# Two pools for the operands of an output projection, its first products in another order, and the keys of two key halves loaded into tiles that are free

## The chip, the core and the metric

The kernel runs on one core of one Trainium2 chip, in one launch. The metric is device time in microseconds (us). The kernel before takes 1855.24 us, the median of 3 runs (1855.01 to 1856.59). The engines are PE (TensorE, matrix products), DVE (VectorE), ACT (ScalarE), POOL (GpSimd) and SP (SyncE, which here only issues DMA transfers). ACT issues transfers as well, and such an issue stands in ACT's own instruction order.

## The reference, cut to what matters

One layer of a hybrid diffusion transformer, float32: 512 latent tokens of width 1024, 256 context tokens.

```python
def reference(x, c, ctx, ...):
    z, xbc, dtr, pl, q, k, v = project(h, sh1, sc1, norm1_g, w_in)
    ssd_l = ssd_mixer(...)                      # 512 x 1024
    na  = neighbourhood_attention(q, k, v, kc, vc, rpb)     # 512 x 512
    mix = concatenate([ssd_l, pool_mixer(pl, ...), na]) @ w_out   # 512 x 2048 @ 2048 x 1024
    h = h + g1 * mix
    u = rmsnorm(h, norm2_g) * (1 + sc2) + sh2
    h = h + g2 * peer_ffn(u, peer_wq, peer_keys, peer_u, peer_v)
    return rmsnorm(h, final_g)

def peer_ffn(u, w_q, sub_keys, u_tab, v_tab):
    q = (t @ w_q).reshape(n_tok, 8, 2, 128)
    s = einsum('thid,hikd->thik', q, sub_keys)  # 16 key halves of 128 keys each
    v1, i1 = top_k(s[:, :, 0], 16); v2, i2 = top_k(s[:, :, 1], 16)
    ...  # 16 of the 256 pairs per head and token, then softmax, gelu(u_tab[idx] . u), sum of v_tab[idx]
```

## The kernel before

A float32 product A·B is done as three fast products: each operand is split into a high part (fp32r; ACT, `split`, L177) and a low part, which is what the high part leaves (a subtraction, L180, on DVE or POOL), and high·high, high·low and low·high are summed in PSUM (`mm3`, L187 to L189; the trace names the operands in the other order). The names end in `h` and `l`: `wh` and `wl` are the parts of a 512 KB piece of weights, which SP loads into a tile `wraw` (L208).

**Output projection beside attention.** The mixed rows have three sources. The SSD part is normalised and transposed on PE, DVE writes it (L910, tiles `y` and `xsn`), SP stores it to `mix_d` in DRAM (L914), and it is loaded again (`s` items) and split into `mAh`, `mAl`. The pooled part lies in `mix_d` already; it is loaded in two pieces (`p4`, `p5`) and split into the first half of `mBh`, `mBl`. Attention writes the second half of those tiles. Tiles `h` (the residual, 4 loads of 512 KB from `x`, L1193), `g1r`, `mBh`, `mBl`, `mAh` and `mAl` are in one pool, `o1`. The pool reaches over the place where `xsn` lay, so the first write to it waits until `xsn` has been stored.

The order of instructions is written by hand: `at(step, f)` puts a piece of work at a step, `before` puts it ahead of what is there, and `run` issues steps 61 onward (`O0 = A0 = 61`) one by one. An engine takes its instructions in that order. Attention takes a pair of heads and a column group (`m` = 0 to 15) every 4 steps: scores (L1026), minimum (L1035, L1036), exponential (L1043), division (L1048, L1049, every second one on POOL), transposes (L1056), copy (L1061), values (L1074). Its biases `nb` are loaded by ACT (L967), its values `vl` by SP (L1015). Between them stand `i_high` and `i_low`, the splits of the next item (`w4, p4, p5, w5, s0, ...`), and `o_part(kk, t)`: 6 products (two halves of a 256-row piece, three each) for 128 tokens and one piece `kk` of `w_out`. The pieces come in the order 4, 5, 0, 1, 2, 3, the four `o_part(4, t)` at steps 62, 62, 63 and 64. A low part that is done frees the item's `wraw`, and the next load waits for that.

**Norm and the step to PEER.** After the output projection, `norm2` (L1250) scales each 128 tokens, `norm2_T` transposes (L1258), `norm2_split` splits into `u2h` and `u2l` in two halves (`q4`). `u_block` computes the products `pu` with 128-expert pieces of `peer_ut`. `q_part` computes a query half (24 products). Two Gelu results `otmp` are stored to `act_d` by ACT (L1363). Then `scores(hi, pq)` (L1406 to L1413): ACT loads the 128 keys of key half `hi`, copies the query half into `qk`, PE multiplies (L1411), ACT copies into `sc`, DVE picks the best 16. `keys`, `qk` and `sc` lie in pool `sc1`, over the place of the tiles `otmp`. `idxG`, `gG` (128 x 128) and `mod`, `cst` are tiles that exist at this time. Up to the end PE then works through the 128 expert pieces (`pu` and `pv`, from about 650 us).

Of the kernel before, what the change touches and what calls it, by code (L numbers as in the profile page):

```python
# [7 lines left out]
F32 = mybir.dt.float32  # L8
F32R = mybir.dt.float32r
# [3 lines left out]
AF = mybir.ActivationFunctionType  # L13
# [4 lines left out]
P = 128  # L18
D = 1024
# [131 lines left out]
def build(tc, A, out, dbg=None):  # L151
# [4 lines left out]
    def dump(name, ap):  # L156
        if name in dbg:
            nc.sync.dma_start(dbg[name], ap)
# [16 lines left out]
    def split(hi, lo, full, eng=None, lows=None):  # L175

        S.activation(hi, full, AF.Copy)  # L177

        def low():
            (eng or V).tensor_tensor(lo, full, hi.bitcast(F32), ALU.subtract)  # L180
        if lows is None:
            low()
        else:
            lows.append(low)
# [474 lines left out]
    def at(step, f, *a):  # L659
        plan.setdefault(step, []).append((f, a))  # L660
# [310 lines left out]
    def i_high(i):  # L971
        kind, n = items[i]
        raw = iraws.pop(i)
        if kind == "w":
            ispls[n] = wspl(raw, 2, None, ilows)
        elif kind == "p":
            ks = slice(2 * n - 8, 2 * n - 6)
            split(mix["h"][:, ks, :].rearrange("p k t -> p (k t)"), mix["l"][:, ks, :].rearrange("p k t -> p (k t)"), raw, None, ilows)
        else:
            ts_ = slice(n * P, (n + 1) * P)  # L980
            split(mix["ah"][:, :, ts_], mix["al"][:, :, ts_], raw.rearrange("p (k t) -> p k t", k=8), None, ilows)
# [131 lines left out]
    ws.extend(wop, "O", 1, 2, "right")  # L1113
    op = Pools()
    o1 = op.sb("o1", side="right")
    pso = Pools()
    psO = pso.ps("psO", bufs=4)
    h = o1.tile([P, NX, D], F32, name="h")
    g1r = o1.tile([P, D], F32, name="g1r")
    mBh = o1.tile([P, 8, SEQ], F32R, name="mBh")  # L1120
    mBl = o1.tile([P, 8, SEQ], F32R, name="mBl")
    mAh = o1.tile([P, 8, SEQ], F32R, name="mAh")
    mAl = o1.tile([P, 8, SEQ], F32R, name="mAl")

    def row_bc(dst, ps_of, bank, j0):

# [6 lines left out]
    def out_mm(acc, w, kk, t, first, last):  # L1133
        for k2 in range(2):
            k = kk * 2 + k2
            mh, ml, kx = (mAh, mAl, k) if k < 8 else (mBh, mBl, k - 8)
            mm3(acc, mh[:, kx, t * P:(t + 1) * P], ml[:, kx, t * P:(t + 1) * P],
                w[0][:, k2, :], w[1][:, k2, :], first and k2 == 0, last and k2 == 1)
# [10 lines left out]
        at(O0 + OI[i], i_low, i)  # L1149
    at(O0 + 66, row_bc, g1r, lambda: psS.tile([P, 512], F32, name="sps"), 1, 0)  # L1150

    def o_part(kk, t):
        if kk == 4:
            accs[t] = psO.tile([P, 512], F32, name="acc")
        out_mm(accs[t], ispls[kk], kk, t, kk == 4, False)
    for j, kk in enumerate((4, 5, 0, 1, 2, 3)):
        for t in range(NX):
            n = 4 * j + t
            at(O0 + ((1, 1, 2, 3)[n] if n < 4 else 6 + (n - 4) * 61 // 19), o_part, kk, t)
    for step in range(O0, max(plan) + 1):  # L1160
        run(step)
    assert not plan
# [26 lines left out]
    psT3 = o2p.ps("psT3", bufs=1, side="right")  # L1189
    ssq = o2.tile([P, NX, 2], F32, name="ssq2")  # L1190

    for t in range(NX):
        nc.scalar.dma_start(h[:, t, :], A["x"][t * P:(t + 1) * P, :])  # L1193
    n2row = o2.tile([P, D], F32, name="xn", bufs=2)
    nc.scalar.dma_start(n2row, A["rowg"][:, 0:D])
    bcr = o2.tile([P, D], F32, name="bcr")
# [74 lines left out]

    def norm2_split(t, q4):
        ks, ts_ = slice(q4 * 4, q4 * 4 + 4), slice(t * P, (t + 1) * P)
        split(u2h[:, ks, ts_], u2l[:, ks, ts_], ufs[q4], V if q4 or t > 1 else G)

    wq, wqs = {}, {}
    for m in range(2):
# [1 line left out]
    for m in range(2):  # L1279
        e_fetch(AHEAD[m], 0)  # L1280
    wqs[0] = wspl(wq[0], KB, G)

    def head(t):
        h_mul(t)
# [17 lines left out]
    def q_part(m, c, ks=range(KB)):  # L1302
        for k in ks:
            mm3(pqs[m][:, c], wqs[m][0][:, k, :], wqs[m][1][:, k, :], u2h[:, k, c], u2l[:, k, c], k == 0, k == KB - 1)
# [53 lines left out]
    G.tensor_tensor(u2G, u2G, bcr2, ALU.add)  # L1358
    for m in range(2):
        q_part(m, late)  # L1360
        act = o2.tile([P, 512], F32, name="otmp", bufs=2)[:, :TD]
        S.activation(act, pus[m][:, :TD], AF.Gelu)
        nc.scalar.dma_start(act_d[m], act)  # L1363
    dump("u2h", u2h.bitcast(F32))
    dump("u2G", u2G)
    order.close()
# [35 lines left out]

    def scores(hi, pq):

        keys = sc1.tile([P, P], F32, name="keys", bufs=2)
        nc.scalar.dma_start(keys, A["keys"][:, hi * P:(hi + 1) * P])  # L1406
        qk = sc1.tile([P, 512], F32, name="qk", bufs=2)
        S.activation(qk, pq, AF.Copy)
        ps = psO.tile([P, 512], F32, name="acc")
        for t in range(NX):  # L1410
            PE.matmul(ps[:, t * P:(t + 1) * P], qk[:, t * P:(t + 1) * P], keys, start=True, stop=True)  # L1411
        sc = sc1.tile([P, NX, P], F32, name="sc", bufs=4)
        S.activation(sc, ps.rearrange("p (t k) -> p t k", t=NX), AF.Copy)  # L1413
        if "sc" in dbg:
            nc.sync.dma_start(dbg["sc"][:, :, hi, :], sc)
        hh, i = hi // 2, hi % 2
        for t in range(NX):
            top16(vv_[t][:, hh, i, :], ix_[t][:, hh, i, :], sc[:, t, :], P, sc2)
        if hi in PAIRS:
            for t, h0, nh in PAIRS[hi]:  # L1420
                top_pairs(t, h0, nh)
# [470 lines left out]
```

## Time and profile before

| what | value |
|---|---|
| median of 3 runs | 1855.24 us (1855.01 to 1856.59) |
| the profiled execution | 1855.9 us, span 1854.1 us, mean granted clock 0.988 |
| PE busy | 1796.4 us, 97% of the span |
| DVE, ACT, POOL busy | 1348.2, 842.0, 390.8 us (73%, 45%, 21%) |
| DMA | 451.46 MB, mean 243 GB/s |

The profile shows one execution. "Busy" is the time in which an engine had an instruction at work; matmul ends are modelled. PEclk is the clock that TensorE was granted, in tenths or as a share of 2.4 GHz, so 0.5 is 1.2 GHz. A row of a timeline gives start, duration, engine and line, what is written from what, and in brackets how long the engine was idle before and what ended that. "ACTq" and "SPq" are DMA issues on those engines' queues. The chain of waits follows the work that ended last back from the end.

### The profile page before, as it was taken

How to read it: one execution, taken by the hardware profiler on the slowest of the kernel's cores; microseconds unless marked ns; L12 is line 12 of the kernel's file. 1: busy time of each engine (PE TensorE's matmuls, PEld its weight loads, DVE VectorE, ACT ScalarE, POOL GpSimd, SP SyncE). 2: the span in 40 equal slices, each digit the busy share in tenths (PEclk: the TensorE clock that was granted, in tenths of full speed). 3: DMA queues.
4: the chain of work that ended last, by engine and by line, in shares of the span. 5: the costliest groups of instructions: out<-in, count | busy, mean ns of one | idle time of the engine just before them, and what ended most of it. 6: DMA issues, size and time to landing. Idle time of an engine off the chain costs nothing.

```text
span 1854.1 us, 26298 instructions
## 1 busy us (share of the span) xinstructions
PE 1796.4 (97%) x9703; PEld 1517.7 (82%) x9703; DVE 1348.2 (73%) x2574; ACT 842.0 (45%) x1493; POOL 390.8 (21%) x276
## 2 busy tenths in 40 slices
PE   6999999998999899999999999999999999999997
PEld 4677776655677788999999998888888888888885
DVE  5554128785643558988989996988888878888876
ACT  4433216544653433345766774444444344444434
POOL 1101300142222544420111111211111111111103
PEclk9999999998999999999999999999999999999999
DMA  9545422118432533365889999999999999999971
GB/s 364 174 142 167 118 103 73 47 57 262 130 109 91 160 116 111 123 225 198 305 330 349 361 338 348 398 353 343 362 344 349 338 350 388 347 351 346 365 249 56
DMA packets 190369, 451.46 MB, mean 243 GB/s; under 512 B 13568, under 2 KB 117248, under 8 KB 172288
## 3 DMA queue, kind: packets, MB, share of 16 engines
q1 hardware_dynamic: 146032, 257.42, 40.5%
q0 software_dynamic: 18576, 136.32, 19.0%
q10 hardware_dynamic: 25632, 56.04, 8.1%
q8 instruction: 76, 1.25, 0.3%
q14 instruction: 53, 0.43, 0.1%
HBM read 397.17 MB, written 54.66 MB: 244 GB/s over the span
## 4 chain that ended last, share of the span: by engine, by line
PE 89%; DVE 3%; ACT 3%; DMA 3%; issue 1%; POOL 1%; ACTq 0%; SPq 0%; DVEq 0%; POOLq 0%
PE pu L187 10%; PE pu L189 10%; PE pu L188 10%; PE pv L189 9%; PE pv L188 9%; PE pv L187 9%; PE acc L187 5%; PE acc L188 5%; PE acc L189 5%; PE acc L402 2%; PE acc L404 2%; PE acc L406 1%; PE gdps L1611 1%; PE gdps L1612 1%; PE sps L1026 1%
## 5 line engine op out<-in xcount | busy, mean ns | idle before, releaser
L180 DVE TENSOR_TENSOR wl<-wraw,wh 128x1024 fp32r<-128x1024 f32 x290 | 355.5, 1238 | 187.9 <-ACT wh L177 181.4
L177 ACT ACTIVATE wh<-wraw 128x1024 fp32r<-128x1024 f32 x324 | 336.8, 1052 | 218.7 <-PE acc L188 74.4
L187 PE MATMUL pu<-u2h,wh 128*128 128x384 f32 x1024 | 349.8, 342 | 0.0
L189 PE MATMUL pu<-u2h,wl 128*128 128x384 f32 x1024 | 345.4, 337 | 0.0
L188 PE MATMUL pu<-u2l,wh 128*128 128x384 f32 x1024 | 344.8, 337 | 0.0
L1550 POOL DMA_INDIRECT row<-in_peer_uv,idxG x128 | 156.7, 1224 | 807.2 <-DVE accG L1564 713.2
L188 PE MATMUL pv<-wl,wwh 128*128 128x512 f32 x768 | 300.7, 392 | 2.3 <-DVE wl L180 2.2
L187 PE MATMUL pv<-wh,wwh 128*128 128x512 f32 x768 | 301.7, 393 | 0.4 <-ACT wh L177 0.3
L189 PE MATMUL pv<-wh,wwl 128*128 128x512 f32 x768 | 300.9, 392 | 0.0
L188 PEld LDWEIGHTS pu<-u2l,wh 128*128 128x128 f32 x1024 | 192.5, 188 | 2.1 <-DVE u2l L180 0.3
L187 PEld LDWEIGHTS pu<-u2h,wh 128*128 128x128 f32 x1024 | 192.3, 188 | 1.8
L189 PEld LDWEIGHTS pu<-u2h,wl 128*128 128x128 f32 x1024 | 192.2, 188 | 0.7 <-DVE wl L180 0.5
L188 PEld LDWEIGHTS pv<-wl,wwh 128*128 128x128 f32 x768 | 144.2, 188 | 34.1 <-DVE wl L180 3.8
L189 PEld LDWEIGHTS pv<-wh,wwl 128*128 128x128 f32 x768 | 144.2, 188 | 32.2
L187 PEld LDWEIGHTS pv<-wh,wwh 128*128 128x128 f32 x768 | 144.2, 188 | 31.2 <-ACT wh L177 1.3
L1564 DVE SCALAR_TENSOR_TENSOR accG<-row,wG,accG 128x1024 f32<-128x1024 f32 x127 | 162.5, 1279 | 4.5 <-ACT wG L1559 3.3
L1555 DVE CUSTOM_DVE_ANT_0 row<-row,u2G 128x1024 f32<-128x1024 f32 x128 | 155.1, 1219 | 0.0
L177 ACT ACTIVATE wwh<-acl 128x384 fp32r<-128x384 f32 x86 | 45.2, 526 | 204.1 <-DVE acl L1723 140.9
L1614 ACT ACTIVATE stg<-gdps 128x512 f32<-128x512 f32 x96 | 101.3, 1169 | 19.4 <-PE gdps L1612 14.9
L180 POOL TENSOR_TENSOR wl<-wraw,wh 128x1024 fp32r<-128x1024 f32 x34 | 81.5, 2400 | 110.4 <-ACT wh L177 73.5
L1717 ACT ACTIVATE act<-pu 128x384 f32<-128x384 f32 x42 | 20.6, 490 | 156.1 <-PE pu L189 142.0
L1344 ACT ACTIVATE act<-pu 128x384 f32<-128x384 f32 x84 | 41.0, 488 | 97.9 <-PE pu L189 77.0
(401 smaller groups left out, 3120.7 us busy)
## 6 DMA issues: line engine op xcount, KB each, us to landing
wraw<-in_peer_ut SPq DMA_DIRECT2D x128, 512.0 KB
wraw<-in_peer_uv SPq DMA_DIRECT2D x128, 512.0 KB
gd<-gd_d SPq DMA_DIRECT2D x15, 1536.0 KB
gd_d<-stg ACTq DMA_DIRECT2D x11, 2048.0 KB
wraw<-in_w_in SPq DMA_DIRECT2D x36, 512.0 KB
acl<-act_d SPq DMA_DIRECT2D x86, 192.0 KB
act_d<-act ACTq DMA_DIRECT2D x84, 192.0 KB
kT<-in_ada_w SPq DMA_DIRECT2D x18, 512.0 KB
```

The lines of the kernel that those rows point to most:

```text
L177: S.activation(hi, full, AF.Copy)
L180: (eng or V).tensor_tensor(lo, full, hi.bitcast(F32), ALU.subtract)
L187: PE.matmul(ps, ah, bh, start=start, stop=False)
L188: PE.matmul(ps, ah, bl, start=False, stop=False)
L189: PE.matmul(ps, al, bh, start=False, stop=stop)
L402: PE.matmul(px, h[:, k, :], uh[:, k, :], start=s, stop=False)
L404: PE.matmul(px, h[:, k, :], ul[:, k, :], start=False, stop=False)
L1344: S.activation(act, pu[:, :TD], AF.Gelu)
L1550: G.indirect_dma_start(out=rows[k], out_offset=None, in_=A["peer_uv"], in_offset=bass.IndirectOffsetOnAxis(ap=idxG[:, k:k + 1], axis=0))
L1555: V.tensor_tensor_reduce(row[:, 0:D], row[:, 0:D], u2G, 1.0, 0.0, ALU.mult, ALU.add, actG[:, k:k + 1])
L1564: V.scalar_tensor_tensor(accG, row[:, D:2 * D], wG[:, k:k + 1], accG, ALU.mult, ALU.add)
L1614: S.activation(stg[:, :, t0:t0 + 4].rearrange("p a t -> p t a"), ps, AF.Copy, scale=1.0 / GSCALE)
```

## The change

In `i_high`, the low part of `p4` goes to POOL. Pool `o1` keeps `h`, `g1r`, `mAh`, `mAl`; `mBh` and `mBl` get a pool of their own, `o1b`, which lies lower and not over `xsn`. The four `o_part(4, t)` are replaced by `o_first`: at step 62 the 16 products with `mBh`, at step 63 the 8 with `mBl`. The four loads of `h` go from the code behind this stage to steps 73 to 76 within it. The low part of `norm2_split(1, 0)` goes from POOL to DVE. The keys of halves 0 and 1 are loaded into `idxG` and `gG` ahead of the norm, their query halves are copied into `mod` and `cst` behind both Gelu, and `scores` takes them from there. The other 14 key halves stay as they were.

```diff
@@ i_high
-            split(mix["h"][:, ks, :]..., mix["l"][:, ks, :]..., raw, None, ilows)
+            split(mix["h"][:, ks, :]..., mix["l"][:, ks, :]..., raw, G if n == 4 else None, ilows)
@@ pools
     o1 = op.sb("o1", side="right")
+    h = o1.tile([P, NX, D], F32, name="h")
+    g1r = o1.tile([P, D], F32, name="g1r")
+    mAh = o1.tile([P, 8, SEQ], F32R, name="mAh")
+    mAl = o1.tile([P, 8, SEQ], F32R, name="mAl")
+    o1b = op.sb("o1b", side="right")
+    mBh = o1b.tile([P, 8, SEQ], F32R, name="mBh")
+    mBl = o1b.tile([P, 8, SEQ], F32R, name="mBl")
...
-    h = o1.tile([P, NX, D], F32, name="h")
-    g1r = o1.tile([P, D], F32, name="g1r")
-    mBh = o1.tile([P, 8, SEQ], F32R, name="mBh")
-    mBl = o1.tile([P, 8, SEQ], F32R, name="mBl")
-    mAh = o1.tile([P, 8, SEQ], F32R, name="mAh")
-    mAl = o1.tile([P, 8, SEQ], F32R, name="mAl")
@@ output projection
+    def o_first(low):
+        for t in range(NX):
+            ts_ = slice(t * P, (t + 1) * P)
+            if not low:
+                accs[t] = psO.tile([P, 512], F32, name="acc")
+            for k2 in range(2):
+                if low:
+                    PE.matmul(accs[t], mBl[:, k2, ts_], ispls[4][0][:, k2, :], start=False, stop=False)
+                else:
+                    PE.matmul(accs[t], mBh[:, k2, ts_], ispls[4][0][:, k2, :], start=k2 == 0, stop=False)
+                    PE.matmul(accs[t], mBh[:, k2, ts_], ispls[4][1][:, k2, :], start=False, stop=False)
     def o_part(kk, t):
-        if kk == 4:
-            accs[t] = psO.tile([P, 512], F32, name="acc")
-        out_mm(accs[t], ispls[kk], kk, t, kk == 4, False)
-    for j, kk in enumerate((4, 5, 0, 1, 2, 3)):
+        out_mm(accs[t], ispls[kk], kk, t, False, False)
+    at(O0 + 1, o_first, False)
+    at(O0 + 2, o_first, True)
+    for j, kk in enumerate((5, 0, 1, 2, 3)):
         for t in range(NX):
-            n = 4 * j + t
-            at(O0 + ((1, 1, 2, 3)[n] if n < 4 else 6 + (n - 4) * 61 // 19), o_part, kk, t)
+            at(O0 + 6 + (4 * j + t) * 61 // 19, o_part, kk, t)
+    for t in range(NX):
+        at(O0 + 12 + t, nc.scalar.dma_start, h[:, t, :], A["x"][t * P:(t + 1) * P, :])
...
-    for t in range(NX):
-        nc.scalar.dma_start(h[:, t, :], A["x"][t * P:(t + 1) * P, :])
@@ norm2_split
-        split(u2h[:, ks, ts_], u2l[:, ks, ts_], ufs[q4], V if q4 or t > 1 else G)
+        split(u2h[:, ks, ts_], u2l[:, ks, ts_], ufs[q4], V if q4 or t else G)
@@ keys
     wqs[0] = wspl(wq[0], KB, G)
+    keys01, qk01 = [idxG.bitcast(F32), gG], [mod[:, 0, :], cst[:, C_U:C_U + 512]]
+    for m in range(2):
+        nc.scalar.dma_start(keys01[m], A["keys"][:, m * P:(m + 1) * P])
...
     for m in range(2):
         q_part(m, late)
+    for m in range(2):
         act = o2.tile([P, 512], F32, name="otmp", bufs=2)[:, :TD]
         S.activation(act, pus[m][:, :TD], AF.Gelu)
         nc.scalar.dma_start(act_d[m], act)
+    for m in range(2):
+        S.activation(qk01[m], pqs[m], AF.Copy)
@@ scores
-        keys = sc1.tile([P, P], F32, name="keys", bufs=2)
-        ...
+        if hi < 2:
+            keys, qk = keys01[hi], qk01[hi]
+        else:
+            keys = sc1.tile([P, P], F32, name="keys", bufs=2)
+            ...
```

**ACT at the start of attention, before.** `mBh<-wraw` is the split of `p4`, the second of them that of `p5`, `wh<-wraw` the last row that of `w5`; brackets name the semaphores that an instruction waits for, those of DMA queues begin with DMAHW.

```order
L697 ACTIVATE qT<-acc 128x8x4x16 [waits PE_49]
L177 ACTIVATE mBh<-wraw 128x1024 [waits DMAHW3_49,DMAHW2_49,DMAHW4_49,DMAHW1_49,DMAHW5_49,DMAHW0_49,DMAHW6_49,DVE_49,Activation_49]
L1193 DMA h<-in_x 128x1024 x2
L1043 ACTIVATE pr,sm<-sps,mn 128x512 [waits DVE_49,Activation_49]
L967 DMA nb<-in_nabias 128x256 [waits DMAHW7_49]
L1043 ACTIVATE pr,sm<-sps,mn 128x512 [waits DVE_49]
L177 ACTIVATE mBh<-wraw 128x1024
L177 ACTIVATE wh<-wraw 128x1024 [waits DMAHW5_49]
```

The same place of the changed kernel:

```order
L697 ACTIVATE qT<-acc 128x8x4x16 [waits PE_49]
L177 ACTIVATE mBh<-wraw 128x1024 [waits DMAHW4_49,DMAHW3_49,DMAHW5_49,DMAHW2_49,DMAHW6_49,DVE_49,Activation_49]
L1043 ACTIVATE pr,sm<-sps,mn 128x512 [waits DVE_49,Activation_49]
L967 DMA nb<-in_nabias 128x256
L1043 ACTIVATE pr,sm<-sps,mn 128x512 [waits DVE_49]
L177 ACTIVATE mBh<-wraw 128x1024 [waits DMAHW7_49]
L177 ACTIVATE wh<-wraw 128x1024 [waits DMAHW5_49,DMAHW1_49,DMAHW6_49,DMAHW0_49,PE_49]
```

The two queues DMAHW1 and DMAHW0, which carry the last two stores of `xsn`, have left the split of `p4` and stand at the split of `w5`; the loads of `h` have left this place.

**PE at the same place, before.** Scores of `m` = 0, then the first two of the eight groups of three:

```order
L1026 MATMUL sps<-kT,qT 128x256 x4
L187 MATMUL acc<-wh,mBh 128x512
L188 MATMUL acc<-wl,mBh 128x512
L189 MATMUL acc<-wh,mBl 128x512
L187 MATMUL acc<-wh,mBh 128x512
L188 MATMUL acc<-wl,mBh 128x512
L189 MATMUL acc<-wh,mBl 128x512
```

In the changed kernel PE has the last of the sixteen products with `mBh`, then those with `mBl` and the scores of `m` = 1 like this:

```order
L1162 MATMUL acc<-wh,mBh 128x512
L1163 MATMUL acc<-wl,mBh 128x512
L1160 MATMUL acc<-wh,mBl 128x512 x8
L1026 MATMUL sps<-kT,qT 128x256 x4
L1056 MATMUL pt<-cst,pr 128x128 x8
```

The number of products is the same, 24; the first that needs `mBl` is the seventeenth and was the third.

**ACT between the Gelu results and the scores, before.** The last row but one of the group is the copy of scores 0; `qk` are the query halves 0 and 1.

```order
L1362 ACTIVATE otmp<-pu 128x384
L1363 DMA act_d<-otmp 128x384
L177 ACTIVATE wh<-wraw 128x1024
L1406 DMA keys<-in_keys 128x128
L1408 ACTIVATE qk<-acc 128x512
L1406 DMA keys<-in_keys 128x128
L1408 ACTIVATE qk<-acc 128x512
L177 ACTIVATE wh<-wraw 128x1024
L1413 ACTIVATE sc<-acc 128x512
L1406 DMA keys<-in_keys 128x128
```

The changed kernel has here:

```order
L1379 ACTIVATE otmp<-pu 128x384
L1380 DMA act_d<-otmp 128x384
L177 ACTIVATE wh<-wraw 128x1024
L1382 ACTIVATE mod<-acc 128x512
L1428 DMA keys<-in_keys 128x128 x2
L177 ACTIVATE wh<-wraw 128x1024
L1382 ACTIVATE cst<-acc 128x512
L1435 ACTIVATE sc<-acc 128x512
```

The two `keys` issues are now those of halves 2 and 3, behind the copy of query half 0 (`mod`); the loads of halves 0 and 1 stand some 30 rows earlier on ACT.

## Rows read from the trace of the kernel before

**Rows 1.** The page: the chain that ended last, by engine.

```profile
PE 89%; DVE 3%; ACT 3%; DMA 3%; issue 1%; POOL 1%; ACTq 0%; SPq 0%; DVEq 0%; POOLq 0%
```

**Rows 2.** Windows: us, busy of PE, PEld, DVE, ACT, POOL, then PEclk, DMA share, GB/s.

```profile
444.00:451.00 7.00, 6.80 (x16) 4.87 (x17) 4.98 (x11) 2.61 (x6) 1.57 (x1) 0.52 0.97 356
628.70:634.50 5.80, 0.00 (x0) 0.00 (x0) 0.00 (x0) 1.74 (x3) 3.98 (x2) 0.75 1.00 286
634.50:638.50 4.00, 3.92 (x13) 3.53 (x14) 1.16 (x8) 0.60 (x1) 4.00 (x3) 0.51 1.03 316
650.00:1850.00 1200.00, 1189.33 (x6501) 1068.70 (x6500) 1003.01 (x1926) 568.79 (x943) 241.93 (x170) 1.00 0.81 298
```

**Rows 3.** Timelines of PE, ACT, DVE and SP, 439 to 452 us.

```profile
439.68 1.13 PE L1026 MATMUL sps<-kT,qT 64*128 64x256 f32 x8 [0.25 <-ACT qT L697]
444.16 0.79 PE L187 MATMUL acc<-wh,mBh 128*128 128x512 f32 x1 [3.35 <-ACT mBh L177]
...
439.03 0.60 ACT L697 ACTIVATE qT<-acc 128x512 f32<-128x512 f32 x1 [2.39 <-PE acc L189]
443.05 1.06 ACT L177 ACTIVATE mBh<-wraw 128x1024 fp32r<-128x1024 f32 x1 [3.43 <-DMA mix_d<-xsn]
451.28 1.06 ACT L177 ACTIVATE wh<-wraw 128x1024 fp32r<-128x1024 f32 x1 [2.37 <-DMA wraw<-in_w_out]
...
440.07 1.22 DVE L180 TENSOR_TENSOR wl<-wraw,wh 128x1024 fp32r<-128x1024 f32 x1
...
445.39 0.37 SPq L208 DMA_DIRECT2D wraw<-in_w_out  x1
```

**Rows 4.** The chain that ended last, 440 to 457 us: start, us, what.

```profile
440.23 2.60 DMA mix_d<-xsn
...
448.35 0.43 PE acc L189
...
452.74 0.23 PE acc L188
...
453.21 1.06 PE sps L1026 x8
...
454.89 0.60 ACT pT L1061
...
455.64 0.63 PE pt L1056 x4
```

**Rows 5.** The page: the costliest groups, low parts on POOL.

```profile
L180 POOL TENSOR_TENSOR wl<-wraw,wh 128x1024 fp32r<-128x1024 f32 x34 | 81.5, 2400 | 110.4 <-ACT wh L177 73.5
```

**Rows 6.** Line L1193, the loads of `h`: count, shortest, median and longest issue in ns.

```profile
L1193 ACTq DMA_DIRECT2D h<-in_x x4: 334/446/455, 443.1 to 455.7; - x4
```

**Rows 7.** PE's waits from 590 to 650 us: total, times, longest.

```profile
PE acc L1411 <- DMA keys<-in_keys: 5.9, 1, 5.9
PE acc L188 <- POOL u2l L180: 1.0, 1, 1.0
```

**Rows 8.** The chain that ended last, 624 to 643 us.

```profile
624.64 3.14 DMA act_d<-otmp
627.92 6.30 DMA keys<-in_keys
...
634.58 2.05 PE acc L1411 x8
...
643.00 0.89 PE acc L1411 x8
```

**Rows 9.** Timelines of DVE and PE, 624 to 629 us.

```profile
624.27 2.79 DVE L180 TENSOR_TENSOR wl<-wraw,wh 128x1024 fp32r<-128x1024 f32 x1 [1.40 <-ACT wh L177]
...
628.40 0.28 PE L189 MATMUL acc<-u2h,wl 128*128 128x256 f32 x1
```

**Rows 10.** Tile `u2l`, 596 to 625 us: shortest, median and longest ns, first and last start.

```profile
L180 DVE TENSOR_TENSOR u2l<-uf,u2h x6: 679/680/2572, 601.3 to 622.2; 128x512 fp32r<-128x512 f32 x6
L180 POOL TENSOR_TENSOR u2l<-uf,u2h x2: 1272/1280/1287, 599.6 to 605.4; 128x512 fp32r<-128x512 f32 x2
```

More of the change, by code (lines that the diff above doesn't have):

```diff
@@ L977, in i_high @@
             ks = slice(2 * n - 8, 2 * n - 6)
-            split(mix["h"][:, ks, :].rearrange("p k t -> p (k t)"), mix["l"][:, ks, :].rearrange("p k t -> p (k t)"), raw, None, ilows)
+            split(mix["h"][:, ks, :].rearrange("p k t -> p (k t)"), mix["l"][:, ks, :].rearrange("p k t -> p (k t)"), raw, G if n == 4 else None, ilows)
         else:
@@ L1403, in scores @@
     def scores(hi, pq):
-        keys = sc1.tile([P, P], F32, name="keys", bufs=2)
-        nc.scalar.dma_start(keys, A["keys"][:, hi * P:(hi + 1) * P])
-        qk = sc1.tile([P, 512], F32, name="qk", bufs=2)
-        S.activation(qk, pq, AF.Copy)
+        if hi < 2:
+            keys, qk = keys01[hi], qk01[hi]
+        else:
+            keys = sc1.tile([P, P], F32, name="keys", bufs=2)
+            nc.scalar.dma_start(keys, A["keys"][:, hi * P:(hi + 1) * P])
+            qk = sc1.tile([P, 512], F32, name="qk", bufs=2)
+            S.activation(qk, pq, AF.Copy)
         ps = psO.tile([P, 512], F32, name="acc")
```

## The prediction

> **What bounds the kernel now.** I read first the page's chain by engine: PE holds 89% of it [rows 1]. So time is gained where PE stands still, or runs at its lower clock. Then I read the windows. From 650 to 1850 us PE is busy 1189.33 of 1200 us at clock 1.00 with a DMA share of 0.81 [rows 2]: an earlier start of that stretch comes out whole at the end, and nothing in it waits for a date. What is left are the waits before it, by PE's timeline and its list of waits.
>
> The first place is at 441 us. PE ends the scores of m = 0 at 440.81 (439.68 + 1.13) and then stands for 3.35 us, released by ACT's `mBh` [rows 3]. ACT itself had been idle since 439.63 and was held 3.43 us by the stores `mix_d<-xsn` [rows 3], the last of which is in the chain at 440.23 for 2.60 us [rows 4]. Behind the wait the granted clock is 0.52 from 444 to 451 us, the lower level of 1.2 GHz [rows 2], and a product takes 0.43 us there against 0.23 us later [rows 4]. So this place costs the idle time and then some of the work behind it. The next scores start at 453.21 [rows 4].
>
> The second is at 629 us. Query half 1 ends at 628.68 (its last product starts at 628.40 and takes 0.28 [rows 9]), and PE stands 5.89 us for the keys [rows 7]: the chain shows the store of `act_d` for 3.14 us, then the keys for 6.30 us [rows 8]. ACT held the keys' load until the store had landed, because `keys` lies over `otmp`. The transfer of 64 KB took that long beside full queues (share 1.00 [rows 2]). Again the clock behind is 0.51 [rows 2].
>
> A third, of 1.0 us, is for `u2l` on POOL [rows 7].
>
> **First place: pool, low part, order of products.** The split `mBh` of `p4` no longer waits for the `xsn` stores, so it follows `qT` on ACT: 439.63 to 440.70 (1.06 us [rows 3]). The first product can start at 440.81. The second needs `wl`, which DVE ends at 441.29 [rows 3]. From there 23 products at the high level's 0.23 us [rows 4] end at 441.33 + 5.29 = 446.62. That holds if `mBl` is there for the seventeenth, at 441.33 + 15 x 0.23 = 444.8. POOL takes 2.40 us for such a low part [rows 5]: 440.70 + 2.40 = 443.1, up to 443.8 with a slow start, so 1.0 to 1.7 us to spare. On DVE it would have stood in front of the minima of m = 0. The scores of m = 1 start at 446.62 in place of 453.21: 6.6 us less, 3.35 of them idle time less the short wait for `wl`, the rest lower clock.
>
> What is late next is `w5`. Its load waits for the buffer that `mBl` frees. Before, it was issued at 445.39 and ACT's split started at 451.28, 5.9 us later, still held 2.37 us by the load [rows 3], which on PE cost nothing, since the products lasted to 453.21. Now it is issued at 443.1 to 443.8 and stands in the same queue behind an `s0` and a `vl` load, while the first two loads of `h`, 1.05 MB, are gone from this window. At 356 GB/s [rows 2] those are 2.9 us. So it lands between 443.2 + 3.0 = 446.2 and 443.8 + 5.9 = 449.7. The wait on the `xsn` stores now stands at this split too; they land at 442.83 (440.23 + 2.60 [rows 4]), earlier than that. Queued behind the split on ACT is `pT`, for which PE's second transposes wait: split 1.06, `pT` 0.60, issue 0.14 (455.64 less 455.49 [rows 4]) make landing + 1.80. Without the wait those transposes would start 2.43 us behind the scores (455.64 less 453.21 [rows 4]), at 449.05. A landing at 446.2 costs 0, at 449.7 costs 2.4. I take 448.2, in the later half because two loads stand ahead, which costs 1.0. First place: **5.6 us** less, bounds 4.2 and 6.6.
>
> **The loads of `h`.** Four issues of 0.33 to 0.46 us [rows 6] leave ACT here and come back 12 steps on, each behind a semaphore of an earlier transfer. Nothing but later work needs `h`. They stand in front of exponentials and `pT`, so a wait in them holds attention. Bounds: 0 where the earlier transfer has long landed, 2.5 where one of the four waits as long as ACT did for `w5` (2.37 [rows 3]). I take **0.3** us lost, near the low end, since at the old place no row shows PE waiting for an issue.
>
> **Second place: keys.** The keys of halves 0 and 1 are loaded some 40 us ahead, so 6.30 us of transfer leave the chain [rows 8]. Query half 0 is ready before half 1 ends, its copy stands on ACT ahead of the loads that still wait for `act_d`, and scores 0 can start at 628.68 itself. At the high clock they take 0.89 us, as the row of scores 1 at 643.00 shows (2.05 at 634.58, at the low one [rows 8]). Query half 2 follows with 24 products at 0.23 us (5.5), and scores 1 start at 628.68 + 0.89 + 5.5 = 635.07 in place of 643.00: **7.9 us** less. Does something else hold PE? `wl` for half 2 is ready at 627.06 (624.27 + 2.79 [rows 9]). ACT is held by the store of `act_d` until 627.78 (624.64 + 3.14 [rows 8]) as before, now for the keys of half 2, and behind that stand the split for the next expert piece (1.06) and the copy of half 1; its low part on POOL (2.40 [rows 5]) ends near 632.9, PE needs it at 635.1. The cover is 2 us; were it gone by as much, the gain would be 5.9. Bounds 5.9 (the idle time alone, with the lower clock as before) and 7.9.
>
> **The norm's low part.** DVE takes 0.68 us for it and POOL 1.28 [rows 10], so PE's wait of 1.0 us can shrink by 0.6; but DVE then reaches the normalisation later by 0.68, and a later low part on DVE took 2.57 us beside POOL [rows 10], on which PE waits next. I count **0**, bounds -0.6 and +0.7.
>
> **The sum.** 5.6 - 0.3 + 7.9 + 0 = 13.2 us less. The profiled execution took 1855.9, so 1842.7; the median lies 0.66 below that execution, so **1842.0 us**.
>
> A rule of the Trainium skill speaks against one part. The row says that a low part of the same kind on DVE took 0.68 us in the median and 2.57 at most [rows 10], the long one while POOL had a low part under way. The "GPSIMD Engine Reference", section "Key points", says that GpSimd shares its SBUF interfaces with VectorE, with contention when VectorE has two SBUF inputs; both subtractions here have two. By that, `mBl` on POOL and `wl` on DVE could hold each other up.
>
> **Rivals.**
> 1. *DVE and POOL hold each other.* `wl` (DVE, 440.07) and `mBl` (POOL, 440.70) overlap for 0.6 us. If DVE were held until POOL is done, the second product would wait for 443.1 + 1.2, that is 444.3 in place of 441.3, PE would idle 3 us as before and the clock would fall as before (24 products, some 15 at 0.43). Then the first place gains about 0.5, and the time is 1855.24 - 0.5 + 0.3 - 7.9 = 1847.1. For it: the 2.57 us row. Against: `wl` starts before `mBh` is done, so DVE is first, and 2.40 on POOL [rows 5] as a mean includes such neighbours. 0.08.
> 2. *`w5` is no earlier.* Its landing is set by what the DMA engines carry, share 0.97 [rows 2], and it comes at 451.2 as before. Then transposes start at 451.28 + 1.80 = 453.1 in place of 449.05, 4.0 lost, and the first place gains 2.6: 1855.24 - 2.6 + 0.3 - 7.9 = 1845.0. For it: the full share. Against: the issue is 2 us earlier and 1.05 MB lighter. 0.12.
> 3. *The other side.* Each of the moved loads of `h` waits on ACT, in order, for an earlier transfer. Were each as long as the longest in this trace (6.30 us [rows 8]), ACT would be held 25 us within four steps, attention stands, and the time is 1842.0 + 25.2 = 1867.2. It decides from a hold of 13.2 us that reaches PE. Against: the earlier transfers were issued several steps before, and old issues took 0.46 us [rows 6]. 0.02.
> 4. *The second place stays held.* `sc` and the later keys still wait for the `act_d` store; if scores 0 were held by it or by the copies behind it, the early keys would be a transfer hidden for nothing: 1855.24 - 5.3 = 1849.9. For it: the 3.14 us in the chain [rows 8]. Against: the store lands at 627.78, ahead of 628.68. 0.05.
>
> **How the numbers follow.** The forecast has 0.73: 1842.0. With every term at its good end it is 1.9 lower (1.0 for `w5`, 0.3 for the issues, 0.6 for the norm), 1840.1; with every term at its bad end 6.3 higher (1.4, 2.2, 2.0, 0.7), 1848.3. The rivals have 0.08, 0.12, 0.02 and 0.05. The range of 8 in 10 takes in the first two rivals and nearly all of these bounds, and goes 1.1 us below them, since PE still idles 10.7 us past 650 (1200 less 1189.33 [rows 2]), of which loads that start earlier could take some: 1839.0 to 1848.0. A measurement of this kernel tells 0.2%, 3.7 us, from no change, so faster is below 1851.5. All cases but the third are, with their bounds; faster 0.95, same 0.03, slower 0.02.
>
> **What would show it.** In the profile after: `mBh` starts at 439.6 with no wait on `mix_d<-xsn`; PE's idle time before the first product with `mBh` is below 0.6 us and the granted clock from 441 to 447 is near 1.0; scores of m = 1 at 446.6; `mBl` on POOL 2.4 us; the second transposes at 449 to 451.5 with `w5` in front; no wait on `keys` at 628, the clock there 1.0; scores 1 at 635 less what the first place gave. PE's waits past 650 us stay near what they are, 1200 us less 1189. The prediction is wrong if the first product still waits over 2 us, if `pT` waits on a load of `h`, or if the gap reopens at the first expert pieces.

## The result, and the profile after

The changed kernel takes 1840.5 us (median of 4 runs, 1839.16 to 1843.9) against 1855.12 us before (4 runs, 1852.22 to 1856.59): ratio 0.9927, 95% interval 0.991 to 0.9943. It is faster, by 10.6 to 16.7 us; 1842.0 was predicted. In a second series it took 1844.58 us against 1855.0, 10.4 us less, ratio 0.9947 (0.9935 to 0.996).

The profiled execution took 1839.16 us, its span is 1837.1 us, 17.0 less than before. To find where the 17.0 us come from, both profiles are cut at three events that each has: the start of the scores of m = 0 (where the change begins), the end of query half 1, and the start of scores 1.

| stretch | before | after | difference |
|---|---|---|---|
| start to scores of m = 0 | 439.68 | 434.65 | -5.03 |
| to the end of query half 1 | 189.00 | 184.33 | -4.67 |
| to scores 1 | 14.16 | 6.23 | -7.93 |
| to the end of the span | 1211.3 | 1211.9 | +0.6 |

The first and the last line lie outside the two places. What they are is settled by the experiments, e3 above all: chance.

**First place.** PE's timeline of the changed kernel, which answers to [rows 3]:

```profile
434.65 1.13 PE L1026 MATMUL sps<-kT,qT 64*128 64x256 f32 x8 [0.25 <-ACT qT L697]
435.71 0.49 PE L1162 MATMUL acc<-wh,mBh 128*128 128x512 f32 x1
436.31 0.51 PE L1163 MATMUL acc<-wl,mBh 128*128 128x512 f32 x1
...
439.91 2.02 PE L1160 MATMUL acc<-wh,mBl 128*128 128x512 f32 x8
441.86 1.14 PE L1026 MATMUL sps<-kT,qT 64*128 64x256 f32 x8
442.93 0.66 PE L1056 MATMUL pt<-cst,pr 128*128 128x128 f32 x4
445.76 0.63 PE L1056 MATMUL pt<-cst,pr 128*128 128x128 f32 x4 [2.17 <-ACT pT L1061]
```

The rows of before for the same two events, the scores of m = 1 and the second transposes:

```profile
453.14 1.13 PE L1026 MATMUL sps<-kT,qT 64*128 64x256 f32 x8
455.64 0.63 PE L1056 MATMUL pt<-cst,pr 128*128 128x128 f32 x4 [0.78 <-ACT pT L1061]
```

The wait of 3.35 us in front of the products is gone. The scores of m = 1 start 7.21 us after those of m = 0 (441.86 less 434.65), 13.46 before (453.14 less 439.68). What is new is the 2.17 us in the last row of the changed kernel. ACT and POOL in the same place, and the chain that ended last:

```profile
434.49 1.05 ACT L177 ACTIVATE mBh<-wraw 128x1024 fp32r<-128x1024 f32 x1
444.07 1.06 ACT L177 ACTIVATE wh<-wraw 128x1024 fp32r<-128x1024 f32 x1 [4.27 <-DMA wraw<-in_w_out]
445.03 0.58 ACT L1061 ACTIVATE pT<-pt 128x512 f32<-128x512 f32 x1
...
435.62 2.89 POOL L180 TENSOR_TENSOR mBl<-wraw,mBh 128x1024 fp32r<-128x1024 f32 x1 [7.78 <-ACT mBh L177]
```

```profile
435.62 2.90 POOL mBl L180
438.54 5.35 DMA wraw<-in_w_out
```

The split of `p4` has no wait on `xsn` any more. The low part on POOL frees the buffer, `w5` is loaded into it, and until it lands ACT holds `pT` behind the split of `w5`.

**Second place.** PE of the changed kernel, from the last product of query half 1 to scores 1, and scores 1 of before:

```profile
618.70 0.28 PE L189 MATMUL acc<-u2h,wl 128*128 128x256 f32 x1
618.82 1.06 PE L1433 MATMUL acc<-idxG,mod 128*128 128x128 f32 x8
...
625.21 1.06 PE L1433 MATMUL acc<-gG,cst 128*128 128x128 f32 x8
```

```profile
642.84 1.05 PE L1411 MATMUL acc<-keys,qk 128*128 128x128 f32 x8
```

Query half 1 ends at 618.98 (618.70 + 0.28), and scores 1 follow after 6.23 us; before, 642.84 less 628.68 is 14.16. The tables of this part count from such timeline rows. The prediction took 453.21 and 643.00 from the chain, for the same events.

The windows over both places, with the columns of [rows 2], and the loads of `h`, which answer to [rows 6] (the line is now that of `run`, which issues the steps):

```profile
435.70:442.70 7.00, 6.89 (x34) 5.13 (x32) 4.34 (x11) 2.51 (x5) 4.39 (x2) 1.00 0.89 283
618.80:625.40 6.60, 6.60 (x36) 5.62 (x35) 3.64 (x25) 2.26 (x4) 4.62 (x3) 1.00 1.07 327
630.00:1830.00 1200.00, 1191.77 (x6512) 1070.77 (x6510) 1003.75 (x1934) 568.89 (x941) 244.43 (x171) 1.00 0.82 299
```

```profile
L667 ACTq DMA_DIRECT2D h<-in_x x4: 334/334/373, 455.4 to 459.0; - x4
```

From 618.80 PE has no idle time, and the clock is at its higher level, 1.00, in both places where it was 0.52 and 0.51. The third window is the long stretch of expert pieces; the section on the prediction comes back to it. PE's waits from 560 to 640 us answer to [rows 7]: the one for the keys is gone, the one for POOL's low part has become two for DVE.

```profile
PE pu L188 <- DVE u2l L180: 0.8, 1, 0.8
PE acc L188 <- DVE ssq L1260: 0.4, 1, 0.4
PE pt L1270 <- DVE xn L1262: 0.2, 1, 0.2
```

### The profile page after: what moved, and what is told of

It is laid out like the page before. It is cut to its first block, busy times and chain, and to the rows that moved or that the text cites. A ratio compares the mean times of both kernels' runs of the same rounds, so it can differ in the third digit from the quotient of the medians.

```text
span 1837.1 us, 26312 instructions
## 1 busy us (share of the span) xinstructions
PE 1787.2 (97%) x9703; PEld 1511.0 (82%) x9703; DVE 1347.4 (73%) x2574; ACT 842.8 (46%) x1493; POOL 393.1 (21%) x276
## 4 chain that ended last, share of the span: by engine, by line
PE 88%; DMA 3%; ACT 3%; DVE 3%; issue 2%; POOL 1%; SPq 0%; ACTq 0%; DVEq 0%; POOLq 0%
PE pu L187 9%; PE pu L189 9%; PE pu L188 9%; PE pv L188 9%; PE pv L189 9%; PE pv L187 9%; PE acc L187 5%; PE acc L189 5%; PE acc L188 5%; PE acc L402 2%; PE acc L404 2%; PE acc L406 1%; PE gdps L1633 1%; PE gdps L1634 1%; PE sps L1026 1%
```

## The experiments

Times scatter: the 12 runs of e1 lie between 1844.87 and 1858.53 us, so a difference of 1 or 2 us is not read from medians. Each run has a profile, and in it the same events are found. The table gives them in us: the start of the scores of m = 0; counted from there, the scores of m = 1, the second transposes and the end of query half 1 ("half 1"); counted from that end, scores 1; then the median, and the ratio to runs of before in the same series (medians 1853.77 to 1855.12) with its interval.

| run | m = 0 | m = 1 | transposes | half 1 | scores 1 | median | ratio |
|---|---|---|---|---|---|---|---|
| before | 439.68 | 13.46 | 15.96 | 189.00 | 14.16 | 1855.12 | |
| changed | 434.65 | 7.21 | 11.11 | 184.33 | 6.23 | 1840.50 | 0.9927 (0.991, 0.9943) |
| e3 (changed again) | 438.33 | 7.20 | 10.94 | 184.14 | 6.22 | 1844.58 | 0.9947 (0.9935, 0.996) |
| e1 first place alone | 437.68 | 7.20 | 10.92 | 183.90 | 14.23 | 1850.54 | 0.9979 (0.9965, 0.9993) |
| e2 keys alone | 439.49 | 13.03 | 15.53 | 188.58 | 6.22 | 1846.85 | 0.996 (0.9946, 0.9973) |
| e9 one pool | 436.81 | 12.89 | 15.39 | 188.75 | 6.22 | 1847.30 | 0.9966 (0.9951, 0.998) |
| e5 old order | 434.62 | 10.67 | 13.17 | 188.09 | 6.22 | 1845.47 | 0.9951 (0.9929, 0.9974) |
| e6 `h` at its old place | 440.54 | 7.21 | 13.75 | 188.74 | 6.23 | 1846.77 | 0.9956 (0.994, 0.9973) |
| e4 low part on DVE | 438.95 | 7.21 | 11.88 | 186.18 | 6.23 | 1842.51 | 0.9932 (0.9919, 0.9945) |
| e13 (e4 again) | 435.97 | 7.21 | 11.07 | 184.22 | 6.23 | 1839.60 | one run |
| e7 norm on POOL | 439.07 | 7.21 | 11.09 | 184.02 | 6.23 | 1843.23 | 0.9941 (0.992, 0.9961) |
| e10 `w5` first | 438.00 | 7.19 | 9.69 | 183.05 | 6.23 | 1842.10 | 0.9936 (0.9911, 0.9961) |
| e11 `w5` first, DVE | 438.38 | 7.21 | 9.71 | 183.06 | 6.22 | 1840.87 | 0.9921 (0.9902, 0.9941) |
| e12 `w5` first, norm on POOL | 439.32 | 7.21 | 9.71 | 182.82 | 6.22 | 1840.34 | 0.9921 (0.9907, 0.9936) |

### Two halves of the change, and the changed kernel again

e1 takes the early keys and the norm's move out of the changed kernel:

```diff
-        split(u2h[:, ks, ts_], u2l[:, ks, ts_], ufs[q4], V if q4 or t else G)
+        split(u2h[:, ks, ts_], u2l[:, ks, ts_], ufs[q4], V if q4 or t > 1 else G)
...
-    keys01, qk01 = [idxG.bitcast(F32), gG], [mod[:, 0, :], cst[:, C_U:C_U + 512]]
...
-        if hi < 2:
-            keys, qk = keys01[hi], qk01[hi]
...
```

> The change's first place alone (two pools, low part of p4 on POOL, products with the low part last, loads of h moved); keys, query copies and the norm's low part as in the kernel before. Theory (the two places add up): from the start of the scores of m = 0 to those of m = 1 7.2 us as in the changed kernel (13.5 before); from m = 0 to the end of query half 1 some 4.7 us less than before; the wait of 5.9 us for the keys and the low clock behind it unchanged. Time 4 to 5 us below before, 7 to 8 above the changed kernel. Rival (the change moved something ahead of this place as well, 5.0 us in the two profiles): the scores of m = 0 start at 434.7 again and the time is near 1845. Rival (the first place's gain is given back in the wait for the keys, whose transfer shares the DMA queues): the wait grows by some us and the time stays within 2 us of before.

Half 1 ends 5.1 us earlier after m = 0 than before (183.90 against 189.00), and the keys still hold PE. PE's waits from 590 to 640 us in e1:

```profile
PE acc L1423 <- DMA keys<-in_keys: 5.3, 1, 5.3
PE acc L188 <- POOL u2l L180: 1.0, 1, 1.0
```

Scores 1 follow half 1 after 14.23 us, 14.16 before: nothing of the first gain was given back there. The median is 4.5 us below before, by the ratio 1.3 to 6.5. The m = 0 scores start at 437.68, so the first rival, that the change brings 5 us ahead of this place, does not hold.

e2 puts only the early keys (the `+` lines of the change from `keys01` to `scores`) into the kernel before.

> The change's second place alone: early keys of halves 0 and 1, query copies in mod and cst; all else as before. Theory: the first place costs what it did (13.5 us between the scores of m = 0 and 1), no wait for keys, and scores 1 start 6.4 us after query half 1 ends in place of 14.3. Time 7.9 us below before, about 1847. Rival (5.0 us came ahead of the first place by the change of tiles): scores of m = 0 start near 439.7 here, and only kernels with two pools start them near 434.7.

Scores 1 follow half 1 after 6.22 us; the wait before the first products is 3.35 us as before. The first place is untouched here, and still m = 1 comes at 13.03 and half 1 at 188.58, where before has 13.46 and 189.00: two products fewer run at 0.43 us, which nothing in this edit explains. So the first gain is known to some 0.4 us. The median is 8.2 us below the 1855.0 of before, by the ratio 5.0 to 10.0. In the profiles the two halves add up: 5.1 us at half 1 in e1 and 7.9 from there to scores 1 in e2 make 13.0, and the changed kernel has 4.67 + 7.93 = 12.6. The medians don't show it so closely: e1 and e2 give 4.5 + 8.2 = 12.7 us, the changed kernel in the same series (e3) 10.4, by the ratio 7.4 to 12.1.

e3 is the changed kernel without an edit.

> The changed kernel once more, on the same chip as the others. Theory (what lies ahead of the first place is the same work in both and differs by chance): the scores of m = 0 start anywhere between 434 and 440 us, later in an execution whose clock dips between 334 and 417 us; the part from there on is as in its first profile: 184.3 us to the end of query half 1, 6.4 us from there to scores 1. Rival: 434.7 us again, as a property of the kernel. Time 12 to 15 us below before.

Its m = 0 scores start at 438.33, not 434.65: 3.7 us of chance in one and the same program, ahead of everything that was changed. Two windows in which such executions part, in before (332 and 398 us), in the changed kernel's first profile and in e3:

```profile
332.00:382.00 50.00, 47.33 (x176) 30.96 (x176) 44.28 (x68) 21.10 (x58) 11.03 (x6) 0.93 0.12 32
398.00:417.00 19.00, 18.21 (x67) 12.67 (x68) 15.25 (x20) 5.58 (x11) 11.69 (x8) 0.91 0.18 55
```

```profile
332.00:382.00 50.00, 48.99 (x193) 32.47 (x194) 45.88 (x69) 24.55 (x67) 12.62 (x7) 0.97 0.12 32
394.00:413.00 19.00, 17.66 (x71) 11.87 (x72) 16.11 (x22) 6.65 (x14) 12.57 (x9) 1.00 0.20 66
```

```profile
332.00:382.00 50.00, 48.36 (x180) 31.62 (x181) 44.45 (x68) 22.43 (x63) 12.14 (x7) 0.93 0.12 32
398.00:417.00 19.00, 18.55 (x72) 12.49 (x71) 14.52 (x19) 6.32 (x13) 12.86 (x9) 0.92 0.21 69
```

e3 has before's clock there (0.93, 0.92), the first profile of the same program a higher one (0.97, 1.00). Over all runs of the table this start lies between 434.62 and 440.54. From the scores of m = 0 to scores 1, e3 and the first profile agree within 0.2 us. The stretch behind scores 1, which the first profile had 0.6 us longer than before, took 1210.9 us in e3 (1211.3 before, 1211.9 there), and between 1210.9 and 1212.7 over all runs. The expected time, 12 to 15 us below before, was missed: it was 10.4.

### What the first gain rests on

e9 puts all six tiles back into one pool, `mBh` and `mBl` between `g1r` and `mAh`:

```diff
-    o1b = op.sb("o1b", side="right")
-    mBh = o1b.tile([P, 8, SEQ], F32R, name="mBh")
-    mBl = o1b.tile([P, 8, SEQ], F32R, name="mBl")
+    mBh = o1.tile([P, 8, SEQ], F32R, name="mBh")
+    mBl = o1.tile([P, 8, SEQ], F32R, name="mBl")
```

> The changed kernel with all six tiles in one pool again, mBh and mBl at its start: the split of p4 waits for the last xsn stores as before; low part on POOL, new order, moved loads of h, early keys stay. Theory (the pool is what the first gain rests on): PE waits 3.35 us before the first product, the clock is at its lower level behind it; the low part is ready 3.9 us after the split starts (2.9 on POOL), so the sixteen products cover it; scores of m = 1 at 13 to 13.5 us, transposes at 15.5 to 17, the first place's gain of 4.7 us gone: 1849 or so. Rival (order and POOL alone give part of it): scores of m = 1 below 12 us.

The theory holds, with its numbers a little high: 12.89 us to m = 1, transposes at 15.39, half 1 at 188.75, a median of 1847.30. So this edit alone undone takes back 4.4 to 4.6 us at half 1. PE and POOL in e9, and the window of the 24 products:

```profile
441.30 0.80 PE L1161 MATMUL acc<-wh,mBh 128*128 128x512 f32 x1 [3.35 <-ACT mBh L177]
...
441.38 2.38 POOL L180 TENSOR_TENSOR mBl<-wraw,mBh 128x1024 fp32r<-128x1024 f32 x1 [11.56 <-ACT mBh L177]
```

```profile
441.30:449.70 8.40, 8.40 (x25) 6.39 (x25) 3.26 (x4) 3.29 (x6) 4.84 (x2) 0.66 0.76 231
```

PE is busy all of the 8.40 us, at clock 0.66: the new order hides POOL but not a late `mBh`.

e5 puts the old order back (the four `o_part(4, t)` at steps 62, 62, 63, 64 in place of `o_first`).

> The changed kernel with the first products in the old order again: four o_part(4, t), so that the third product needs the low part of p4 (on POOL, done 3.9 us after the scores of m = 0 start); all else as changed. Theory (the order lets PE work while POOL is busy, and what bounds the place behind it is the load of w5): PE waits about 2 us before the third product, the scores of m = 1 start at 9.0 us after those of m = 0 in place of 7.2, but the second transposes only at 11.4 in place of 10.9, since the split of w5 stands in front of their input anyway: 0.5 us lost of 1.8. Rival (a 2 us wait drops the clock as the 3.35 us did): products at 0.43 us, scores of m = 1 at 13, transposes at 15, the whole first gain gone.

```profile
438.49 0.80 PE L189 MATMUL acc<-wh,mBl 128*128 128x512 f32 x1 [1.71 <-POOL mBl L180]
```

```profile
437.50:443.50 6.00, 5.01 (x15) 4.03 (x16) 2.55 (x6) 2.25 (x5) 2.51 (x2) 0.72 0.99 323
```

The wait is there, 1.71 us, but its consequence was larger than the theory's and smaller than the rival's: the clock did fall (0.72), m = 1 starts at 10.67, and the transposes at 13.17, when `w5` has long been split and hides nothing of the loss. Behind the wait six products take 0.43 us each, the pace of the lower level, and the later ones 0.23. 2.1 to 2.2 us are lost by then. Half 1 ends 3.8 to 4.0 us later; the other 1.7 stand in a window from 494.6 to 534.6 us with clock 0.96, which no wait of this place explains and which may be chance.

e6 puts the loads of `h` back:

```diff
-    for t in range(NX):
-        at(O0 + 12 + t, nc.scalar.dma_start, h[:, t, :], A["x"][t * P:(t + 1) * P, :])
...
+    for t in range(NX):
+        nc.scalar.dma_start(h[:, t, :], A["x"][t * P:(t + 1) * P, :])
```

> The changed kernel with the four loads of h where they were, so that two of them issue behind the second mBh split, about 4.7 us after the scores of m = 0; all else as changed. Theory (the first place is bounded by the landing of w5, and 1.05 MB in front of it or beside it cost what they take at 370 GB/s, 2.8 us, or half of that where they share): w5 lands 1.4 to 2.8 us later, the second transposes start at 12.3 to 13.8 in place of 10.9. Rival (the loads of h run on another queue and w5 is limited by its own): transposes at 10.9 to 11.2, no difference.

The theory's upper end: the transposes come at 13.75. In the chain of e6 the load of `w5` takes 8.15 us (5.35 above), PE waits 4.82 us for `pT`, and the window behind has clock 0.52:

```profile
444.43 8.15 DMA wraw<-in_w_out
```

```profile
454.29 1.09 PE L1056 MATMUL pt<-cst,pr 128*128 128x128 f32 x4 [4.82 <-ACT pT L1061]
```

```profile
452.00:459.00 7.00, 4.71 (x16) 3.53 (x18) 2.78 (x7) 4.42 (x8) 1.56 (x1) 0.52 1.12 338
```

Half 1 ends at 188.74, near the 189.00 of before: this edit alone undone takes back 4.4 to 4.6 us. Two loads on ACT's queue delay one on SP's. That is what the Trainium skill's "DMA: Bandwidth & Descriptors", section "Issuing engines are not separate DMA queues", states: transfers run on the same 16 DMA engines and interleave whichever engine issued them. This run shows it, 8.15 against 5.35 us.

### What is late now: `w5`

e4 gives the low part of `p4` back to DVE (`raw, None, ilows` in place of `raw, G if n == 4 else None, ilows`).

> The changed kernel with the low part of p4 back on DVE, ahead of the minima of m = 0. Theory (what is late at the first place now is the load of w5, which waits for the buffer that this low part frees): the low part ends at 437.4 where POOL's ended at 438.5 (by the first profile's times), the load is issued 1.1 us earlier and lands 1.1 us earlier, and the second transposes start 1.1 us earlier: 10.0 us after the scores of m = 0 in place of 11.1. Time about 1 us below the changed kernel. Rival (POOL is needed so that the minima of m = 0 are not late): exponentials come 1.2 us later and the transposes with them, time 1 us above the changed kernel. Rival (the landing is set by what the DMA engines carry): the transposes start at 11.1 as before, no difference.

`w5` was issued 1.1 us earlier, yet the transposes came later, at 11.88, and half 1 at 186.18. So the theory fell: the load did not land earlier. A second execution:

> The changed kernel with the low part of p4 on DVE, a second execution, since its first showed w5 issued 1.1 us earlier and landing 0.9 us later than with POOL. Theory (a load issued while s1 and vl0 are still under way shares with them and lands later, in every execution): 7 us or more from issue to landing again, second transposes at 11.7 to 12 us, wait of 2.9 us, lower clock behind it. Rival (a single late landing): 5.2 to 5.9 us from issue to landing, transposes at 9.8 to 10.5, no lower clock.

The chains of e4 and of e13, with PE's wait of e4 and a window at the same place of both (12.0 us after m = 0):

```profile
441.73 7.24 DMA wraw<-in_w_out
...
450.83 1.09 PE L1056 MATMUL pt<-cst,pr 128*128 128x128 f32 x4 [2.95 <-ACT pT L1061]
...
450.95:453.95 3.00, 3.00 (x10) 2.43 (x10) 2.06 (x7) 1.94 (x6) 0.47 (x1) 0.50 1.06 331
```

```profile
438.75 6.43 DMA wraw<-in_w_out
...
447.97:450.97 3.00, 3.00 (x17) 2.02 (x16) 1.94 (x8) 2.21 (x4) 1.28 (x1) 1.00 1.03 330
```

7.24 and 6.43 us from issue to landing, in place of 5.2 to 5.35. Neither expectation of e13 came true: the landing was neither 7 us or more behind the issue nor 5.9 or less. In e13 it is the same moment as with POOL (transposes at 11.07 against 10.94 to 11.11), so e4's third expectation, no difference, is what holds. That the load shares longer with the loads ahead fits, but isn't shown by itself. The extra 0.8 us of e4 is one execution's. It made the wait 2.95 us in place of 2.14; the clock behind fell (0.50 in e4, 1.00 in e13), and 0.8 us became 2.0 at the end of half 1. In these profiles POOL or DVE is no matter for the time; e11 below tests it again.

e10 changes only the order of loads on SP: that of `w5` goes ahead of those of `s1` and `vl`:

```diff
-    at(O0, i_load, 3)
     at(O0, i_load, 4)
     before(O0, i_low, 1)
     before(O0, i_high, 1)
+    before(O0, i_load, 3)
```

> The changed kernel with one change on SP: the load of w5 takes the buffer that w4's low part frees and so is issued ahead of the loads of s1 and vl0, 1.6 us after the scores of m = 0 start in place of 3.9. Theory (the wait of 2.0 to 2.2 us before the second transposes is the landing of w5): it lands 5 us after its issue or sooner, by 6.9, its split is done by 8.0, ahead of the transposes' input, the second transposes start at 9.6 in place of 10.9, and the piece w5 is not waited for: 1.3 us less to the end of query half 1, up to 2.0. Rival (the next thing is late: vl0, now behind, or the low part of w5 on DVE): the transposes start at 9.6 but PE waits for another release within 20 us and the end of query half 1 is where it was. Too small for the times alone; read from the trace.

ACT and PE in e10:

```profile
443.84 1.06 ACT L177 ACTIVATE wh<-wraw 128x1024 fp32r<-128x1024 f32 x1 [0.69 <-DMA wraw<-in_w_out]
...
447.69 0.63 PE L1056 MATMUL pt<-cst,pr 128*128 128x128 f32 x4 [0.78 <-ACT pT L1061]
...
465.36 0.63 PE L1056 MATMUL pt<-cst,pr 128*128 128x128 f32 x4 [0.90 <-ACT pT L1061]
```

The split of `w5` is done before `pT` has its input, the wait is the 0.78 us of before, and half 1 ends 1.1 to 1.3 us earlier. The rival shows only in small measure: 18 us later PE waits 0.90 us for `pT`, and the chain there comes from a load of `vl` that took 7.48 us. But the wait of 0.84 us for `wl` of the changed kernel near there is gone. e11 does the same with the low part on DVE:

> The kernel with w5's load first, and the low part of p4 on DVE. Theory (with the low part on DVE alone, w5 landed 0.9 us later although issued 1.1 us earlier, and the wait of 2.95 us behind it brought the lower clock; that is the load, not the 1.1 us by which DVE's minima come later): with w5's load first both are gone, the second transposes start at 9.6 to 9.8 us, no lower clock from 0 to 30 us, the end of query half 1 at 183.0. Rival (the later minima, exponentials and splits behind them are what costs): the transposes start at 10.7 or later and the end of query half 1 is 1 us or more above 183.0.

9.71 and 183.06: the same, so with `w5` first it does not matter which engine has the low part, and in e4 it was the load that was late.

e7 puts the norm's low part back on POOL (the norm hunk of e1 alone):

> The changed kernel with the low part of norm2_split(1, 0) back on POOL. Theory (the move is worth nothing: DVE has it done earlier than POOL, but is then later with the next low part): from the second transposes to the end of query half 1 173.0 us, as in the kernel with the first place alone, in place of 173.2; PE's wait there 1.0 us for POOL again, in place of 0.4 and 0.8 for DVE. Rival (the move brings the 0.6 us that the durations 0.68 and 1.28 promise): 173.8 us.

172.93 us from the transposes to the end of half 1 (184.02 less 11.09) in place of 173.20 and 173.22: the move costs 0.2 to 0.3 us.

e12 is e10 with that hunk, the version that the experiments point to:

> The kernel with w5's load first, and the norm's low part back on POOL, as the version that should beat both kernels. Theory: second transposes at 9.7 us after the scores of m = 0, end of query half 1 at 182.8 (184.1 to 184.3 in the changed kernel, 189.0 before), scores 1 6.2 us later; 1.4 us below the changed kernel, 13.5 to 14 below before where the stretch ahead runs alike. Rival: something later in that stretch takes the 1.3 us back, 184 us.

182.82 us to the end of half 1, as expected: 1.3 to 1.5 below the changed kernel, 6.2 below before, in the shared stretch. The median is 1840.34 us, ratio to before 0.9921 (0.9907 to 0.9936). Against the changed kernel (0.9927 and 0.9947) the intervals overlap; that it is the faster is shown by the stretch in one profile of it, not by the times.

## Why the prediction was right, step by step

- *The wait on `xsn` goes, and the clock with it.* Right. The scores of m = 1 were put 6.94 us after m = 0 (446.62 less 439.68) and came at 7.2: 6.25 gained of the 6.6. e9 shows that it rests on the pool.
- *The low part on POOL is covered.* Right: 2.89 us in place of 2.40, done 3.86 us after m = 0, and its first product starts at 5.26. e5 shows that without the new order it is not covered.
- *`w5` is late next.* Right in place and mechanism, a little small. Its landing was put 8.5 us after m = 0 (448.2) and came at 9.24 (443.89) and 9.08 (e3), within the bounds. The price is 10.9 to 11.1 less 9.7 (e10), 1.3 to 1.4, not 1.0. The load ahead of it is that of `s1`, not of `s0` as the text said.
- *First place, 5.6.* It gave 4.85 to 5.0 at the transposes (15.96 less 11.11 and 10.94) and 4.7 to 5.1 at the end of half 1: mis-sized by two of the terms above, the 6.6 and the price of `w5`.
- *The loads of `h`, 0.3 lost at the new place.* Nothing was lost on PE: from the transposes to the end of half 1 it took 172.98 us with the loads moved (e1) and 173.04 before. ACT is held a little: three of the four issues, 0.34 us or less each, stand in the chain of e3, but it leads to a wait of 0.84 us for `wl` that before has as well, with 0.85. What their move is worth was seen as part of `w5` (1.05 MB, 2.9 us); e6 measured 2.8 us of landing, and 4.4 to 4.6 us with the clock.
- *The keys, 7.9.* 7.93. PE goes on with scores 0 at once. POOL's low part ends 4.2 us after half 1 (620.78 + 2.40 less 618.98), as the text put it (632.9 less 628.68), and is not waited for.
- *The norm, 0.* 0.2 to 0.3 lost, within the bounds: DVE is now waited for twice, 0.4 and 0.8 us.
- *Rivals.* DVE and POOL did meet, but it was POOL that was slower (below), and the new order covered it. The text's argument that the mean of 2.40 us on POOL has such meetings in it does not hold: without one it was 2.38 (e9). `w5` did not land as late as 11.5 us after m = 0. No load of `h` held PE, and `act_d` did not hold scores 0.
- *The range.* Its lower end rests on 10.7 us that PE still idles past 650. Most of that is no wait: PE's last product ends at 1842.07, so 7.9 of it lie behind the end of PE's work, and 2.7 were there to be had. Nothing of them was gained: in the changed kernel's window of 1200 us PE idles 8.2, of which 5.0 lie behind its last product (it ends at 1824.99), so 3.2 ahead of it.

That the median came within 1.5 us of 1842.0 is in part luck: 12.0 us of the profile's 17.0 lie behind m = 0, and 5.0 are chance that the two profiles happened to differ by; in its second series the same program gained 10.4 us in place of 14.6. What the stretches give, 12.6 of the 13.2, is the better measure. What the prediction missed is that the parts of the first place don't add. It gave them separate terms; undone one at a time, the pool, the loads of `h` and the order take back nearly all of it (4.4 to 4.6 us) or close to half (2.1 us at least), because the wait that is left brings the lower clock back (0.66 in the window of e9, 0.52 in e6, 0.72 in e5).

## What to carry to other kernels

Cut both profiles at events that the change doesn't touch and compare stretch by stretch; a whole time with some us of scatter cannot carry a gain of one. When a wait is removed, look on the next queue for what its end used to hide, here a weight load, and try first to issue that one ahead of loads that nobody waits for yet. Where a PE wait is followed by a lower granted clock, price the wait and the clock together; a small wait that remains can cost more than its length, as the 1.71 us of e5 did, which put m = 1 back by 3.5 us.

## What the runs showed of the hardware

Rows of e3 (DVE, POOL) and of before (POOL, and DVE with two of the rows merged); the POOL row of e9 stands above:

```profile
438.72 1.22 DVE L180 TENSOR_TENSOR wl<-wraw,wh 128x1024 fp32r<-128x1024 f32 x1
439.30 2.89 POOL L180 TENSOR_TENSOR mBl<-wraw,mBh 128x1024 fp32r<-128x1024 f32 x1 [7.82 <-ACT mBh L177]
```

```profile
610.62 2.41 POOL L180 TENSOR_TENSOR wl<-wraw,wh 128x1024 fp32r<-128x1024 f32 x1
611.00 3.17 DVE L180 TENSOR_TENSOR u2l<-uf,u2h 128x512 fp32r<-128x512 f32 x2 [0.21 <-ACT u2h L177]
```

- A subtraction of 128 x 1024 on POOL took 2.89 us where it began 0.64 us before DVE's own subtraction of two SBUF tiles ended (e3: 439.30, and 438.72 + 1.22), and 2.38 us in e9, where DVE had no subtraction at the time; DVE's took 1.22 us in both surroundings. The 0.51 us are near the overlap. The Trainium skill's "SBUF — State Buffer", section "SBUF: two separate sides", says that of two such instructions the one that starts first keeps the shared ports and the other waits; this case agrees, here and in the 2.57 us of [rows 10], the first of the two at 611.00, where POOL had begun at 610.62 and DVE was the slower one. Not explained is DVE's division in e9: begun 0.76 us behind POOL's subtraction, it took 1.90 us, against 0.51 in e3.
- A wait's length did not tell alone whether the granted clock falls behind it: after 1.71 us (e5) it fell to the lower level for some products, 0.72 over 6 us; after 2.01 to 2.17 us (e1, e3, e7, e13, changed) it stayed at 1.00; after 2.95 us and more (before, e4, e6, e9) it fell to the lower level. How long it stays there differs too: after the same wait of 3.35 us, 9 products take 0.43 us in e2, 11 before and 12 in e9. Why 1.71 us brought it and 2.17 did not is open.
- A 512 KB load that was issued 1.1 us earlier behind the same two loads did not land earlier (e13) or landed later (e4). Issued 2.3 us earlier and in front of them (e10), its split began 5.8 us after m = 0 in place of 9.3 to 9.4. Why e4's landed 0.8 us later than e13's is open.
